# Memory keys issued earlier, memory weights split further ahead, one block's low part by DMA, and the last norm on VectorE alone

## The chip, the cores and the metric

The kernel runs on one core of a Trainium2 chip. The metric is the device time of one execution in microseconds (us); the verdict compares medians over runs on the same chip. Times inside the kernel are read from one profiled execution and count from its first instruction.

## The reference

Two layers of a hybrid decoder step, for 512 prompt tokens and 8 sequences of 8 sample tokens (576 tokens in all), all in float32. Of each layer:

```
rq, rk, rv, rg, sq, sk, sv, mq, g_r, g_s, g_m = in_proj(x, w_in[l])      # x @ w_in, rotary on rq rk sq sk
ret_o = retention(rq, rk, rv);  swa_o = sliding_window_attention(sq, sk, sv, sinks)
mk, mv = mem_prompt @ w_mem_kv[l]                                       # 256 memory tokens, 4 heads of 128
mem_o  = softmax(mq mk^T / sqrt(128)) mv      # prompt; the samples use cache_mem_k, cache_mem_v (8 sequences)
merged = sigmoid(g_r) * (silu(rg) * gn(ret_o)) @ w_br_ret + sigmoid(g_s) * swa_o @ w_br_swa + sigmoid(g_m) * mem_o @ w_br_mem
x = LN(alpha x + merged @ w_out);  h = relu(x @ w_up)^2;  x = LN(alpha x + h @ w_down)
```

## The kernel before

**Tokens and weights.** Tokens stand in the columns, in two groups A and B of 288 (256 prompt, 32 sample each); a group's product of one 128-wide weight unit is 24 matmuls of 288 columns: every weight and every activation is split into a rounded high part (hi) and a remainder (lo), and the three products hi hi, hi lo and lo hi are added. A *unit* is 1024 x 128 weights (512 KB), 154 a layer, in the order of `unit_order()` (line 67): mk 0 to 3 and mv 0 to 3 (keys and values of the memory, with 256 and 512 columns), then retention (rk, rq, rv, rg), sv, sk, sq, the gates gr with br, mq, the gates gs with bs and gm with bm, wo, up, the MLP in quarters (`ua`, `ub`, `dh`) and dn. In the MLP two weight units and two groups are multiplied as a 2 x 2 block with seven products instead of eight (`pair_steps`, line 657); `block()` (line 570) makes the weights of one of the seven, 128 x 512, by sums of VectorE, a cast on ScalarE (hi) and a subtraction on VectorE (lo).

**Buffers and splitting.** Nearly all tiles share one pool of 38 buffers (`N_T`, tag "T"). A tile whose buffer still has readers makes its first writer wait. `run()` (line 613) goes through a stage's steps in order. Between groups of matmuls each step calls `fill.advance(dt)` (line 404), which moves the plan's clock `fill.t`, lets generators (attention, norms) put their next operations into the engines' queues, and then calls `tick()` (line 594), which may split one more unit: its use must be within LOOK = 24 us, the live weight tiles (two a unit, one a block) must not pass `2 * cap`, and it must be due within LEAD = 13 us, or ScalarE free and the data there. `split()` (line 551) takes one of two ways:

```
if self.use[i] - self.fill.t > FAR and k[1] not in ("mq", "gs", "bs", "gm", "bm") and u > 15 \
        and (k[1] != "dh" or k[2] == 0):
    self.nc.scalar.copy(hi, raw)
    self.nc.scalar.activation(lo, raw, AF.Copy, scale=-1.0)
    self.nc.gpsimd.dma_start(lo, raw, accum_op=ALU.add)      # lo = raw - hi, by DMA
else:
    self.split_into(hi, lo, raw, True)                       # cast, and a subtraction on VectorE
```

with FAR = 11. `feed()` fetches raw weights on SP's queue two units ahead of the split. The generators go on when a modelled clock of the engines (`Clock`, line 268) says that their inputs are ready; engines then run their queues in the order of issue, so the model sets the order and the hardware sets the time.

**Attention to the memory.** `mem_prompt` (line 1350) does one head of the prompt: scores, softmax, transposes (line 1389), and the product with the values. `mem_sample` (line 1418) does four of the sample sequences: it makes masked queries, multiplies four key tiles (in_mck, 512 KB each) in turn, then four value tiles (in_mcv). Two key tiles are loaded ahead by `mem_ahead` (line 1414) and two at `mem_sample`'s own start (line 1430), all on GpSimd's queue. The order is prompt head, ahead, prompt head, sample, twice a layer, within the stages gs/bs and the start of gm/bm. Those left over are run off after the first two gm units.

**Norms.** `norm_ev` (line 838) adds each unit's product to a sum, and `last()` (line 883) then takes the mean, the variance and 1/sqrt, and scales. In layer 1's last norm (`out is None`) GpSimd subtracts the mean from half of the columns (line 902) and does the last of four multiplications (line 916), beside VectorE.

**Stages of layer 1's start.** The norm of group B of layer 0 runs while TensorE does mk and mv of layer 1 and then rk and rq of group A; rk of group B is the first that needs it.

Of the kernel before, what the change touches and what calls it, by code (L numbers as in the profile page):

```python
# [43 lines left out]
CAP_M = 4  # L44
# [405 lines left out]
class Builder:  # L450
# [119 lines left out]
    def block(self, u, b):  # L570


        V = self.nc.vector
        ra, rb = self.raw[u - 1], self.raw[u]
        if b == 1:
            sa, sb = self.tile([P, 8, P]), self.tile([P, 4, P], tag=("s", "rc")[u // 2 % 2], bufs=1)
            self.raw[u, "s"] = sa, sb
            V.tensor_tensor(sa.rearrange("p (e s) c -> p e s c", e=2), ra.rearrange("p (e s) c -> p e s c", e=2),
                            rb[:, 0:4].unsqueeze(1).to_broadcast([P, 2, 4, P]), ALU.add)
            V.tensor_tensor(sb, sa[:, 4:8], ra[:, 0:4], ALU.add)  # L580
        elif b > 1:
            sa, sb = self.raw[u, "s"]
        if b == 6:
            V.tensor_tensor(rb[:, 0:4], sb, rb[:, 4:8], ALU.add)
        src = (ra[:, 0:4], b and sb, b and sa[:, 0:4], b and sa[:, 4:8], rb[:, 4:8], ra[:, 4:8], rb[:, 0:4])[b] \
            if b else ra[:, 0:4]
        w = self.tile([P, 8, P], F32R)
        self.nc.scalar.copy(w[:, 0:4], src)
        V.tensor_tensor(w[:, 4:8], src, w[:, 0:4].bitcast(F32), ALU.subtract)
        if b == 6:  # L590
            del self.raw[u - 1], self.raw[u], self.raw[u, "s"]
        return w[:, 0:4], w[:, 4:8]
# [245 lines left out]
    def norm_ev(self, g, y, l, gi, eps, out, scale=None, bias=1.0):  # L838
# [44 lines left out]
        def last():  # L883
            p1, p2 = self.bank("a")[:, :n], self.bank("a")[:, :n]
            yield from mean(p1, st["acc"])
            yield from mean(p2, st["s2"])
            yield (p1,)
            t = self.tile([P, 288], tag="ln", bufs=2)[:, :n]
            S.activation(t, p1, AF.Square)
            mu = p1  # L890
            if out is None:
                mu = self.u(n)
                S.copy(mu, p1)
            yield (t, p2)
            v, r = self.u(n), self.u(n)
            V.scalar_tensor_tensor(v, p2, eps, t, ALU.add, ALU.subtract)
            r0 = self.tile([P, 288], tag="ln", bufs=2)[:, :n]
            S.activation(r0, v, AF.Ln)
            S.activation(r0, r0, AF.Exp, scale=-0.5)
            mb = mu.unsqueeze(1).to_broadcast([P, 4, n])  # L900
            if out is None:
                G.tensor_tensor(y[1], y[1], mb, ALU.subtract)
            V.tensor_tensor(y[0], y[0], mb, ALU.subtract)
            yield (r0,)
            a = self.tile([P, 288], tag="ln", bufs=2)[:, :n]
            V.tensor_tensor(a, r0, r0, ALU.mult)
            V.scalar_tensor_tensor(a, a, -0.5, v, ALU.mult, ALU.mult)
            V.scalar_tensor_tensor(r, a, 1.5, r0, ALU.add, ALU.mult)
            rb = r.unsqueeze(1).to_broadcast([P, 2, n])
            pieces = [(j, slice(k, k + 2)) for j in range(2) for k in (0, 2)]  # L910

            def mult(i):
                j, k = pieces[i]
                if i == 2 and out is not None:
                    V.tensor_tensor(y[1], y[1], mb, ALU.subtract)
                e = G if i == 3 and out is None else V
                e.tensor_tensor(y[j][:, k], y[j][:, k], rb, ALU.mult)
                return y[j][:, k]

            def affine(q, dst, src, eng):  # L920
                gam, bet = gb(q)
                if eng is S:
                    S.activation(dst, src, AF.Identity, scale=gam, bias=bet)
                else:
                    V.tensor_scalar(dst, src, gam, bet, ALU.mult, ALU.add)

            def end(i):
                j, k = pieces[i]
                for q in (k.start, k.start + 1):
                    affine(4 * j + q, y[j][:, q], y[j][:, q], V)  # L930
                h = out[g]["h"][j][:, k]
                self.pick(y[j][:, k], h).tensor_tensor(out[g]["l"][j][:, k], y[j][:, k], h.bitcast(F32), ALU.subtract)
            if out is not None:
                out[g]["h"] += [self.tile([P, 4, n], F32R) for _ in range(2)]
                out[g]["l"] += [self.tile([P, 4, n], F32R) for _ in range(2)]
            z = [mult(i) for i in range(4)]
            step = 1 if out is None else STEP
            wait = ()
            for i in range(0, 4, step):
                yield wait + tuple(z[i:i + step])  # L940
                for j, k in pieces[i:i + step]:
                    for q in (k.start, k.start + 1):
                        affine(4 * j + q, y[j][:, q] if out is None else out[g]["h"][j][:, q], y[j][:, q],
                               V if out is None and i > 1 else S)
                    if out is None:
                        c = 4 * j + k.start
                        nc.sync.dma_start(self.O["yT"][:, c:c + 2, OFF[g]:OFF[g] + n], y[j][:, k])
                    else:
                        wait = (out[g]["h"][j][:, k],)
                if out is not None:  # L950
                    for e in range(i - step, i):
                        if e >= 0:
                            end(e)
            if out is not None:
                yield wait
                for e in range(4 - step, 4):
                    end(e)
            if gi and out is not None:
                for j in range(2):
                    G.dma_start(self.xs[:, 4 * j:4 * j + 4, OFF[g]:OFF[g] + n], y[j])  # L960
# [386 lines left out]
            lo = SW[g]["l"][0][:, :, cs].rearrange("p g (b t) -> p g b t", b=4)  # L1347
            yield from self.hi_lo(hi, lo, o)

    def mem_prompt(self, h, mq, mk, mv, ME):  # L1350
        nc = self.nc
        V, S, T = nc.vector, nc.scalar, nc.tensor
        ident = self.c("ident")
# [33 lines left out]
        for kb in range(2):  # L1387
            for c in range(4):
                T.transpose(pss[kb][:, c * P:(c + 1) * P], p[:, c, kb * P:(kb + 1) * P], ident)
        del p  # L1390
        pT = [self.tile([P, 2, 512], F32R) for _ in range(2)]
        for kb in range(2):
            yield (pss[kb],)
# [24 lines left out]
    def mem_sample(self, kt, l, f, mq, ME):  # L1418
# [8 lines left out]
        for b in range(4):  # L1427
            V.tensor_tensor(qz[:, b], mq[g][:, :, cs],
                            mm[:, b].unsqueeze(1).to_broadcast([P, 4, 32]), ALU.mult)
        kt += [self.mem_load("mck", l, f * 4 + b) for b in (2, 3)]  # L1430
        vt = []
        ps = self.bank("a")
        for b in range(4):
# [43 lines left out]
    def layer(self, l, X):  # L1477
# [30 lines left out]
        def mv_step(i):  # L1508
            def fn():
                if i == 0:  # L1510
                    mvps[0], mvps[1] = self.bank("g"), self.bank("g")
                hi, lo = self.w[uid["mv", i]]
                hi = hi.rearrange("p (k a) c -> p k (a c)", k=2)
                lo = lo.rearrange("p (k a) c -> p k (a c)", k=2)
                for t in range(2):
                    for k in range(2):
                        kk = 2 * i + k
                        xh = M["h"][kk // 4][:, kk % 4, t * P:(t + 1) * P]
                        xl = M["l"][kk // 4][:, kk % 4, t * P:(t + 1) * P]
                        T.matmul(mvps[t], lhsT=xh, rhs=hi[:, k], start=(kk == 0), stop=False)  # L1520
                        T.matmul(mvps[t], lhsT=xh, rhs=lo[:, k], start=False, stop=False)
                        T.matmul(mvps[t], lhsT=xl, rhs=hi[:, k], start=False, stop=(kk == 7))
                    if t == 0:
                        self.fill.advance(6 * mm_us(512))
                if i == 3:
                    for t in range(2):
                        S.copy(mv[:, t, :], mvps[t])
                    nc.gpsimd.dma_start(self.O["mv"][l], mv)
                    nc.gpsimd.dma_start(mvd, mv)
                    nc.gpsimd.dma_start(mkd, mk)  # L1530
            return ([uid["mv", i]], fn, 6 * mm_us(512))
        steps += [mv_step(i) for i in range(4)]

        def mk_out():
# [7 lines left out]
                S.copy(t, ps)  # L1542
                nc.gpsimd.dma_start(self.O["mk"][l, :, kb], t)
        steps.append(([], lambda: self.fill.add(mk_out(), 2), 0.0))
        self.run(steps, CAP_M)

        GR = {g: {"h": [], "l": []} for g in "AB"}
        xs = self.tile([P, 8, P], F32R)
# [175 lines left out]
        mem = []  # L1724
        for f in range(2):
            kt = []
            mem += [self.mem_prompt(2 * f, mq, mk, mv, ME), self.mem_ahead(kt, l, f),
                    self.mem_prompt(2 * f + 1, mq, mk, mv, ME), self.mem_sample(kt, l, f, mq, ME)]
        for gen in mem:
            self.fill.add(gen, 3)  # L1730

# [15 lines left out]
        for i in range(4):  # L1747
            for m in (2 * i, 2 * i + 1):
                steps += self.both(uid["gs", m], X, gate_ev(m))
            for e in range(2):  # L1750
                steps += self.both(uid["bs", i], SW, add_ev(2 * i + e), range(4 * e, 4 * e + 4))
        self.run(steps)
        del SW
        M2 = self.feat_tiles(2)
        y = {}
# [208 lines left out]
```

## Time and profile before

| | us |
|---|---|
| median of three runs | 2178.79 (2178.54 to 2181.57) |
| profiled execution | 2171.27 |
| its span, first to last instruction | 2169.1 |
| TensorE busy in the span | 2118.1 |
| VectorE busy | 1266.0 |
| ScalarE busy | 931.4 |
| GpSimd busy | 236.2 |

A page shares the span among engines; "PE" is TensorE's matmuls, "PEld" its weight loads, DVE VectorE, ACT ScalarE, POOL GpSimd, SP the queue of weight loads. A busy share near 100% says that only the idle time of that engine can be gained. All instructions carry line 359, that of the helper which records them, so one goes by tiles and by place in time: pg and pa are banks of PSUM, T any tile of the common pool, u, t, ln smaller ones.

### The profile page before, as it was taken

The numbers are of one execution on the slowest core, as the hardware profiler recorded it, in microseconds if no ns is written. First come the engines' busy times: TensorE is split into PE (matmuls) and PEld (weight loads), VectorE is DVE, ScalarE is ACT, GpSimd is POOL, SyncE is SP. The second block draws the span as 40 slices with busy tenths as digits, with TensorE's granted clock in tenths as the row PEclk, the third lists the DMA queues.
The fourth block names the chain that finished last, engine by engine and source line by source line (L and its number), as shares of the span: only waits on it lengthen the run. The fifth ranks groups of instructions, "written<-read, shape, count | busy, mean of one in ns | idle before, by whom it ended". The sixth has DMA issues, their size and how long they took to land.

```text
span 2169.1 us, 39184 instructions
## 1 busy us (share of the span) xinstructions
PE 2118.1 (98%) x16180; PEld 2054.7 (95%) x16180; DVE 1266.0 (58%) x2693; ACT 931.4 (43%) x1758; POOL 236.2 (11%) x292
## 2 busy tenths in 40 slices
PE   9999999999999999999989999999999999999997
PEld 8999999989999999999989999999999999999986
DVE  6455544455557576765755556444555575777767
ACT  4333445232256444445543333562231565444452
POOL 0111210000022000000311111010000220000013
PEclk9999999999999999999999999999999999999998
DMA  8455655434375422224775557444342855223241
GB/s 314 114 142 143 166 120 124 137 98 154 109 209 127 125 96 81 79 88 144 198 217 143 143 142 174 118 118 126 126 149 86 228 117 135 88 79 100 95 117 54
DMA packets 86322, 288.75 MB, mean 133 GB/s; under 512 B 9408, under 2 KB 19136, under 8 KB 86080
## 3 DMA queue, kind: packets, MB, share of 16 engines
q1 hardware_dynamic: 50944, 168.27, 23.0%
q0 software_dynamic: 30112, 110.12, 23.0%
q10 hardware_dynamic: 5088, 7.87, 1.1%
q8 instruction: 127, 2.08, 0.4%
q14 instruction: 51, 0.42, 0.1%
HBM read 200.89 MB, written 15.99 MB: 100 GB/s over the span
## 4 chain that ended last, share of the span: by engine, by line
PE 91%; DVE 4%; issue 2%; ACT 2%; DMA 2%; POOL 0%; SPq 0%; DVEq 0%; POOLq 0%; ACTq 0%
PE pg L359 68%; PE pa L359 22%; DVE T L359 3%; ACT T L359 1%; DMA T<-in_wall 1%; ACT u L359 1%; DVE u L359 1%; DMA T<-in_mck 1%; DMA T<-T 0%; DVE ln L359 0%; DVE accA L359 0%; DVE s L359 0%; POOL T L359 0%; ACT t L359 0%; SPq L359 0%
## 5 line engine op out<-in xcount | busy, mean ns | idle before, releaser
L359 PE MATMUL pg<-T,T 128*128 128x288 f32 (+1 forms) x11840 | 1644.1, 297 | 20.4 <-ACT T L359 15.8
L359 PEld LDWEIGHTS pg<-T,T 128*128 128x128 f32 x11840 | 1592.7, 190 | 46.4 <-ACT T L359 23.4
L359 ACT CAST T<-T 128x1024 fp32r<-128x1024 f32 (+7 forms) x483 | 368.7, 788 | 224.0 <-DVE T L359 174.3
L359 PE MATMUL pa<-T,T 128*128 128x288 f32 (+8 forms) x3368 | 447.7, 303 | 10.4 <-DMA T<-in_mck 6.4
L359 PEld LDWEIGHTS pa<-T,T 128*128 128x128 f32 (+3 forms) x3368 | 395.8, 175 | 32.8 <-issue 9.8
L359 DVE TENSOR_TENSOR T<-T,T 128x512 fp32r<-128x512 f32 (+8 forms) x427 | 370.9, 880 | 92.2 <-ACT T L359 82.8
L359 POOL DMA_DIRECT2D T<-T x136 | 118.7, 883 | 1375.4 <-ACT T L359 963.0
L359 ACT ACTIVATE T<-T 128x1024 fp32r<-128x1024 f32 (+1 forms) x148 | 157.5, 1065 | 10.5 <-DVE T L359 8.2
L359 ACT ACTIVATE t<-pg 128x288 f32<-128x288 f32 x128 | 52.7, 411 | 246.7 <-PE pg L359 246.3
L359 ACT ACTIVATE u<-u 128x288 f32<-128x288 f32 x200 | 89.1, 445 | 95.5 <-DVE u L359 91.4
L359 DVE TENSOR_TENSOR T<-u,T 128x288 fp32r<-128x288 f32 x160 | 72.4, 454 | 78.5 <-ACT T L359 78.5
L359 ACT COPY T<-pg 128x512 f32<-128x512 f32 (+2 forms) x44 | 20.9, 480 | 212.3 <-PE pg L359 212.3
L359 DVE TENSOR_TENSOR T<-T,pg 128x288 f32<-128x288 f32 x128 | 57.7, 451 | 73.9 <-PE pg L359 73.6
L359 DVE TENSOR_TENSOR T<-T,u 128x288 f32<-128x288 f32 (+2 forms) x132 | 90.0, 692 | 4.1 <-ACT T L359 0.5
L359 ACT CAST T<-u 128x288 fp32r<-128x288 f32 x160 | 69.3, 433 | 52.6 <-DVE u L359 48.5
L359 DVE SCALAR_TENSOR_TENSOR T<-t,pg 128x288 f32<-128x288 f32 x64 | 29.0, 453 | 93.9 <-ACT t L359 76.2
L359 DVE TENSOR_TENSOR T<-pa,T 128x512 fp32r<-128x512 f32 (+2 forms) x48 | 25.2, 535 | 76.2 <-ACT T L359 75.8
L359 DVE TENSOR_TENSOR T<-T,pa 128x288 f32<-128x288 f32 (+1 forms) x92 | 52.2, 567 | 24.0 <-PE pa L359 23.2
L359 DVE SCALAR_TENSOR_TENSOR u<-t,pg 128x288 f32<-128x288 f32 x64 | 28.7, 448 | 44.1 <-PE pg L359 44.1
L359 DVE TENSOR_TENSOR u<-u,pa 128x288 f32<-128x288 f32 x72 | 32.6, 453 | 33.0 <-PE pa L359 32.8
L359 ACT CAST T<-pa 128x512 fp32r<-128x512 f32 (+2 forms) x40 | 17.4, 437 | 54.1 <-PE pa L359 50.2
L359 DVE CAST T<-T 128x1024 fp32r<-128x1024 f32 (+1 forms) x52 | 35.8, 689 | 6.8 <-PE pa L359 4.8
(165 smaller groups left out, 1107.1 us busy)
## 6 DMA issues: line engine op xcount, KB each, us to landing
T<-in_wall SPq DMA_DIRECT2D x305, 512.0 KB, 4.1
T<-T POOLq DMA_DIRECT2D x136, 512.0 KB, 5.6
T<-in_mck POOLq DMA_DIRECT2D x16, 512.0 KB, 4.4
T<-in_mcv POOLq DMA_DIRECT2D x16, 512.0 KB, 4.7
T<-in_s POOLq DMA_DIRECT2D x8, 512.0 KB, 8.3
out_state_s<-T POOLq DMA_DIRECT2D x8, 512.0 KB, 4.0
T<-in_xT SPq DMA_DIRECT2D x4, 576.0 KB, 11.5
T<-in_xT ACTq DMA_DIRECT2D x4, 576.0 KB, 6.4
```

The source lines that it names most:

```text
L359: r = f(*a, **kw)
```

## The change

In `block()`, block 5 of the last quarter (key q = 7, two pairs a layer) gets its low part from a second ScalarE pass and an accumulating DMA. In `last()`, with `out is None`, GpSimd's subtraction and multiplication go to VectorE. `mem_prompt` gets a function `ahead`, called behind its transposes: the second head of each pair issues key tiles 2 and 3 there, and `mem_sample` no longer does. In `mv_step` `advance` is called after each 3 matmuls, no longer after each 6. The stage of mk and mv has cap 8 in layer 1 (4 in layer 0, as before), and that of gs and bs has cap 2.5, where it had 3.

```diff
@@ block
-        V.tensor_tensor(w[:, 4:8], src, w[:, 0:4].bitcast(F32), ALU.subtract)
+        if b == 5 and self.items[self.split_next][1][2] == 7:
+            self.nc.scalar.activation(w[:, 4:8], src, AF.Copy, scale=-1.0)
+            self.nc.gpsimd.dma_start(w[:, 4:8], src, accum_op=ALU.add)
+        else:
+            V.tensor_tensor(w[:, 4:8], src, w[:, 0:4].bitcast(F32), ALU.subtract)
@@ norm_ev, last
             if out is None:
-                G.tensor_tensor(y[1], y[1], mb, ALU.subtract)
+                V.tensor_tensor(y[1], y[1], mb, ALU.subtract)
...
-                e = G if i == 3 and out is None else V
-                e.tensor_tensor(y[j][:, k], y[j][:, k], rb, ALU.mult)
+                V.tensor_tensor(y[j][:, k], y[j][:, k], rb, ALU.mult)
@@ mem_prompt(..., ahead=None), behind the transposes
+        if ahead is not None:
+            ahead()
@@ mem_sample
-        kt += [self.mem_load("mck", l, f * 4 + b) for b in (2, 3)]
@@ mv_step
                     for k in range(2):
+                        if t or k:
+                            self.fill.advance(3 * mm_us(512))
...
-                    if t == 0:
-                        self.fill.advance(6 * mm_us(512))
...
-            return ([uid["mv", i]], fn, 6 * mm_us(512))
+            return ([uid["mv", i]], fn, 3 * mm_us(512))
...
-        self.run(steps, CAP_M)
+        self.run(steps, 2 * CAP_M if l else CAP_M)
@@ layer
             kt = []
+
+            def more(kt=kt, f=f):
+                kt += [self.mem_load("mck", l, f * 4 + b) for b in (2, 3)]
             mem += [self.mem_prompt(2 * f, mq, mk, mv, ME), self.mem_ahead(kt, l, f),
-                    self.mem_prompt(2 * f + 1, mq, mk, mv, ME), self.mem_sample(kt, l, f, mq, ME)]
+                    self.mem_prompt(2 * f + 1, mq, mk, mv, ME, more), self.mem_sample(kt, l, f, mq, ME)]
@@ layer, the stage of gs and bs
-        self.run(steps)
+        self.run(steps, 2.5)
```

## Rows read from the trace of the kernel before

**Rows 1.** The page's part 1: busy us, share of span, instructions by engine.

```profile
PE 2118.1 (98%) x16180; PEld 2054.7 (95%) x16180; DVE 1266.0 (58%) x2693; ACT 931.4 (43%) x1758; POOL 236.2 (11%) x292
```

**Rows 2.** Waits of TensorE, whole span: us in total, times, longest.

```profile
PE pg L359 <- ACT T L359: 15.8, 9, 4.6
PE pa L359 <- DMA T<-in_mck: 6.4, 2, 3.3
```

**Rows 3.** Windows: busy us by engine, granted clock, DMA share, GB/s.

```profile
1560.40:1572.70 12.30, 9.24 (x67) 7.57 (x67) 2.58 (x6) 2.02 (x4) 2.11 (x4) 0.72 0.71 255
```

**Rows 4.** Timeline of TensorE, first mem_sample, both layers: start, us, [idle before].

```profile
480.96 1.50 PE L359 MATMUL pa<-T,T 128*32 128x256 f32 x24
485.78 1.08 PE L359 MATMUL pa<-T,T 128*32 128x256 f32 x8 [3.32 <-DMA T<-in_mck]
486.79 5.14 PE L359 MATMUL pg<-T,T 128*128 128x288 f32 x30
...
1560.44 1.50 PE L359 MATMUL pa<-T,T 128*32 128x256 f32 x24
...
1566.01 6.38 PE L359 MATMUL pg<-T,T 128*128 128x288 f32 x30
```

**Rows 5.** Timeline of TensorE, undisturbed: second mem_sample's keys, and 30 matmuls.

```profile
536.04 4.23 PE L359 MATMUL pg<-T,T 128*128 128x288 f32 x30
...
547.17 1.93 PE L359 MATMUL pa<-T,T 128*32 128x256 f32 x32
549.03 1.06 PE L359 MATMUL pg<-T,T 128*128 128x288 f32 x6
```

**Rows 6.** Timeline, layer 0: transposes, GpSimd's late key loads; the chain's landing.

```profile
467.44 1.03 PE L359 MATMUL pa<-cst,T 128*128 128x128 f32 x8
...
477.62 0.53 POOL L359 DMA_DIRECT2D T<-in_mck  x1 [26.02 <-DVE T L359]
...
479.99 0.53 POOL L359 DMA_DIRECT2D T<-in_mck  x1 [1.84 <-PE pg L359]
...
479.99 5.75 DMA T<-in_mck
```

**Rows 7.** Timeline of ScalarE and VectorE: the slowest split in gs and bs.

```profile
507.41 1.06 ACT L359 CAST T<-T 128x1024 fp32r<-128x1024 f32 x1
...
511.55 1.22 DVE L359 TENSOR_TENSOR T<-T,T 128x1024 fp32r<-128x1024 f32 x1
```

**Rows 8.** Timeline, layer 0, last quarter's second pair: VectorE, ScalarE, TensorE.

```profile
1011.95 0.69 DVE L359 TENSOR_TENSOR T<-T,T 128x512 fp32r<-128x512 f32 x1 [1.61 <-ACT T L359]
...
1014.85 0.39 ACT L359 COPY u<-pg 128x288 f32<-128x288 f32 x1
...
1015.29 1.86 PE L359 MATMUL pg<-T,T 128*128 128x288 f32 x12 [1.18 <-ACT u L359]
```

**Rows 9.** DMA view: 1059 to 1068 (GpSimd's queue, landing); 1076 to 1102, tenths.

```profile
q0 software_dynamic: 286, 1.04, 63.9%
...
T<-T POOLq DMA_DIRECT2D x3, 512.0 KB, 5.2
...
DMA  7839988679999999999851898993399999899928
```

**Rows 10.** Timeline, layer 1's start: ScalarE's norm and copy, TensorE's wait.

```profile
1079.83 2.17 ACT L359 ACTIVATE T<-T,par 128x288 fp32r<-128x288 f32 x4
...
1089.42 0.37 ACT L359 COPY T<-pg 128x256 f32<-128x256 f32 x1 [1.56 <-PE pg L359]
...
1112.69 2.16 PE L359 MATMUL pg<-T,T 128*128 128x288 f32 x4 [4.61 <-ACT T L359]
```

**Rows 11.** Timeline of VectorE: 1152 columns alone, and the last norm's two steps.

```profile
2110.89 1.36 DVE L359 TENSOR_TENSOR T<-T,u 128x1152 f32<-128x1152 f32 x1
...
2155.24 3.73 DVE L359 TENSOR_TENSOR T<-T,u 128x1152 f32<-128x1152 f32 x1
...
2160.37 3.30 DVE L359 TENSOR_TENSOR T<-T,u 128x576 f32<-128x576 f32 x3
```

More of the change, by code (lines that the diff above doesn't have):

```diff
@@ L1348, in swa_sample, with mem_prompt @@
             yield from self.hi_lo(hi, lo, o)
-    def mem_prompt(self, h, mq, mk, mv, ME):
+    def mem_prompt(self, h, mq, mk, mv, ME, ahead=None):
         nc = self.nc
```

## The prediction

> **What bounds the kernel now.** I read the busy shares first, then TensorE's waits, then its timeline around each wait, then the other engines and the transfers there. TensorE is busy for 2118.1 of 2169.1 us [rows 1]; the change takes no matmul away, so it can only gain or lose idle time of TensorE (some 36 us, all its waits added up) and the slow clock behind it. Two kinds of wait matter here [rows 2]: 6.4 us, in two waits, for memory keys (in_mck), and 15.8 us in nine for tiles that ScalarE writes, the longest 4.6 us. A wait costs more than its length: over the stretch around the second key wait the mean granted clock was 0.72 [rows 3], that is part of it at 1.2 instead of 2.4 GHz.
>
> **Memory keys.** A mem_sample multiplies four key tiles in a row. In layer 0 three of them start at 480.96 (x24) and the fourth only at 485.78 (x8), and the 30 matmuls behind it take 5.14 us; the same in layer 1, with 6.38 us [rows 4]. Undisturbed, in the second mem_sample, the 32 take 1.86 us (547.17 to 549.03) and 30 such matmuls 4.23 [rows 5]. So layer 0 loses 486.79 - 480.96 - 1.86 = 3.97 plus 5.14 - 4.23 = 0.91, together 4.88 us; layer 1 loses 1566.01 - 1560.44 - 1.86 = 3.71 plus 2.15, together 5.86. Sum 10.7.
> The reason stands in GpSimd's rows: the two late key loads go out at 477.62 and 479.99, each held for a buffer, and the last lands 5.75 us after its issue [rows 6]. The change issues both behind the transposes at 467.44 [rows 6], about 10 us before they go out now; even held for one more unit (48 matmuls at the pace of [rows 5], 6.4 us) the last would be there at 467.4 + 6.4 + 5.75 = 479.6, before 480.96. What is late next is the value loads; they take the buffers that the key matmuls free, and then go out at about 482 to 484. The last, 6 us later, is there at 490, about 1.5 us before it is used. I take all of it: **-10.7**. Bounds: 0 if the buffers are no earlier, -10.7.
>
> **cap 2.5 in gs and bs.** Two tiles' worth less of weights may be live, so a unit is split while the one before it runs, 6.4 us ahead, not two units (12.8). One split is a cast and a subtraction; the longest that I see there starts its cast at 507.41 and ends its subtraction at 511.55 + 1.22 = 512.77, so 5.4 us [rows 7], which fits into 6.4 (the low part is wanted 8 or 16 matmuls later still). I take **+0.5**; bounds 0 and, if each of the 24 units (12 a layer) were 0.5 late, +12.
>
> **Low part of block 5, for the last quarter.** Four blocks (two a layer). Each takes a 0.69 us subtraction and its wait of 1.61 us for ScalarE's cast off VectorE, and puts a second ScalarE pass of about 0.61 and an accumulating transfer of 256 KB in their place [rows 8]. In the second pair of the quarter ScalarE and VectorE wait for each other and run behind TensorE, which then waits 1.18 us for the copy at 1014.85 [rows 8]. Laying ScalarE's list out again without the pause: the two activations before it come 0.6 earlier, right behind the added pass, the pre-add of block 6 on VectorE comes out of the way, and the copy moves to about 14.1: 0.7 us a layer. The first pair shows no such wait and gains nothing. **-1.4**. The transfer is issued at about 1012.5 and wanted at 1018.6; from the 512 KB rows below (2.9 us of transfer in 5.2) a half takes 3.7 to 5, so it is just in time. Bounds: -3 and +3 (a miss of 1.5 a layer).
>
> **Memory weights of layer 1.** Here the trace shows no wait of TensorE for them. What the new cap does is in the code: with cap 4, eight tiles are live at the first mk unit, so a unit is split only when one ends, three short units (3 x 24 matmuls of 0.12, 8.6 us) ahead. That is under FAR (11), so hi goes to a cast and lo to VectorE. With cap 8 nothing blocks, and the split comes when LEAD (13) lets it, 12 to 13 us ahead: over FAR. So mv 0 to 3 and the first rk unit move to the path of two ScalarE passes and an accumulating DMA. VectorE loses five subtractions (6 us there, all beside matmuls). The transfers gain five accumulates, each 63.9% of 9 us for 1.04 MB, so 2.9 us of all 16 engines per 512 KB [rows 9]. They fall in the stretch from 1076 to 1102, in which the engines are busy in most slices at 8 or 9 tenths already [rows 9]: 26 us with some 4 to spare, and 14.5 more. The first mv unit starts at about 1089.3, when the last mk is copied out; ScalarE is held by the norm until 1079.83 + 2.17 = 1082.0 [rows 10], so mv 0's pass ends at 1084, its transfer goes out and lands, at the 5.2 us of [rows 9] with a crowd on the engines, at 1089.5 to 91, and its low part is wanted with the second matmul. Letting the transfers share the engines in their order, I get waits of about 1.6, 0.5 and 1.7 us in mv 0 to 2, and a little slow clock: +4.5. On the other side, the norm of group B gets VectorE earlier. Its wait is the longest of all, 4.61 us before the matmuls at 1112.69 [rows 10], because its last steps stand behind the rotary steps of two projections in VectorE's order. The finer advance may let the first of them go ahead; the rest still comes behind projection A. I give that -2. Together **+2.5**; bounds: -6 (that wait and the slow clock in it gone, no transfer late) and +10.6 (all of the transfer time that doesn't fit, 14.5 - 3.9).
> A rule bears on this: the Trainium skill, DMA: Bandwidth & Descriptors, section on the anatomy of one DMA on the SWDGE path, puts a GpSimd transfer at about 2.0 us plus its bytes over 436 GB/s, an estimate of 3.2 us for 512 KB. By it mv 0 would be there at 1088, no low part would be late, and this part would be -2 and not +2.5. The row says 5.2, for accumulates; I go by the row.
> In layer 0 the added advances change nothing that I can see: TensorE waits for nothing there from 18 to 480 us.
>
> **Last norm on VectorE.** At the end VectorE's subtraction of 1152 columns takes 3.73 us beside GpSimd's; alone the same takes 1.36 [rows 11]. Two in a row are 2.7: -1.0. Three multiplications beside GpSimd's take 3.30 [rows 11]; four of 0.72 take 2.9: -0.4. Nothing else runs there: **-1.5**. Bounds -2 and 0. For group B the same steps run under the last matmuls, and VectorE ends them at the same time as now.
>
> **Sum.** -10.7 + 0.5 - 1.4 + 2.5 - 1.5 = -10.6. The profiled execution took 2171.27 us (span 2169.1), so it would be 2160.7; the median of the runs shown is 7.5 higher, 2178.79, and becomes **2168.2**.
>
> **Rivals.**
> (a) *The layer 1 start pays.* The transfers keep up, and group B's norm goes ahead of the rotary steps: -6 in place of +2.5, so -19.1: 2159.7. For it: VectorE's 6 us less there. Against: [rows 9]. The Trainium skill's rule above speaks for it.
> (b) *The keys are no earlier,* since the 38 buffers are still full at the transposes: -10.7 is lost, and the rest makes about 0: 2178.9. For it: both loads wait for buffers now [rows 6]. Against: cap 2.5 leaves two buffers more, just what two loads take.
> (c) *Weights late in gs and bs:* +12 in place of +0.5: 2179.7. Against: the 5.4 us of [rows 7] is the worst of the stretch.
> (d) *Slower: the transfers of the memory weights.* All 10.6 us come out as waits in mv and the first rk, the clock stays at its lower level through some 8 us of matmuls there, as it did around the key waits [rows 3], which doubles them (+8), and the norm of group B, whose steps stand behind those matmuls, moves along: 18.6 in place of 2.5, and the sum +5.5: 2184.3. The other parts give 13.1, so it decides from a price of 17.5 on. For it: the crowd of [rows 9]. Against: a weight that is late holds TensorE, and the transfers behind it are then wanted later too.
>
> **How the numbers follow.** Forecast 58% (2164 to 2174 its own range), (a) 14, (b) 11, (c) 8, (d) 9. About 0.2%, 4.4 us, is what a measurement of this kernel can tell from none. Faster by more than that: the forecast, (a), and some of the milder (c), 0.74; within it: (b), most of (c), 0.16; slower 0.10. Range: (a)'s end at the low side, 2159.5, and most of the way to (b) and (c) at the high side, 2176.5, which leaves out 2 in 10.
>
> **What would show it.** No wait for in_mck on TensorE in either layer, its four key tiles x32 in one piece, and full clock there. GpSimd's key loads just behind the transposes. ScalarE activations in pairs of 1.05 and five more T<-T issues from GpSimd around 1082 to 1096, with waits of TensorE for DMA T<-T in mv if I am right and none if (a) is. From the last group A mean to the end 1.5 us less, with no GpSimd instruction in it. The forecast is wrong if a wait for in_mck stays, or if gs and bs show waits for ScalarE's or VectorE's weight tiles.

## The result, and the profile after

The kernel after takes 2157.77 us (median of four runs, 2157.64 to 2158.67), the kernel before 2179.95 beside it: a ratio of 0.9899, 95% interval 0.9882 to 0.9916, some 22 us. I had forecast 2168.2, about half of that gain, and a range from 2159.5 to 2176.5; the direction was right, the size and the range were not.

The profiled execution of the kernel after took 2157.69 us, its span 2155.9. TensorE's waits (us in total, times, longest) answer to [rows 2]:

```profile
PE pg L359 <- ACT T L359: 10.9, 7, 2.5
PE pg L359 <- DVE T L359: 3.4, 3, 2.1
...
PE pg L359 <- DMA T<-T: 3.2, 2, 2.9
```

The line for in_mck is gone, ScalarE's longest wait has fallen from 4.6 to 2.5, and the waits for accumulating transfers (T<-T) are 3.2 us, where the kernel before had one of 0.2. The window from layer 1's first key matmuls on, as long as that of [rows 3] and nearly at the same place in the work (columns as there), has no wait and the full clock, where it had 0.72:

```profile
1549.00:1561.30 12.30, 12.30 (x159) 11.19 (x152) 7.18 (x21) 2.02 (x4) 2.10 (x4) 1.00 0.69 257
```

The timeline of GpSimd and TensorE at layer 0's first sample (start, us, instruction, idle before) answers to [rows 4, 6]: both late key loads go out 6.5 us ahead of TensorE's transposes (GpSimd doesn't wait for these), and the 32 key matmuls are one piece.

```profile
460.87 1.05 POOL L359 DMA_DIRECT2D T<-in_mck  x2 [9.20 <-PE pg L359]
...
467.33 1.04 PE L359 MATMUL pa<-cst,T 128*128 128x128 f32 x8
...
478.47 1.94 PE L359 MATMUL pa<-T,T 128*32 128x256 f32 x32
```

So far this reads as the prediction said it would. That it is not the work of the moved loads only the experiments show. At layer 1's start TensorE's timeline answers to [rows 10]:

```profile
1085.68 1.22 PE L359 MATMUL pg<-T,T 128*128 128x512 f32 x2 [2.89 <-DMA T<-T]
1086.70 1.16 PE L359 MATMUL pa<-t,ones 128*128 128x288 f32 x4
...
1111.46 0.53 PE L359 MATMUL pg<-T,T 128*128 128x288 f32 x2 [2.06 <-DVE T L359]
1112.94 3.28 PE L359 MATMUL pg<-T,T 128*128 128x288 f32 x13 [0.95 <-DVE T L359]
```

The first line is mv 0's late low part; the last two are what is left of the 4.61 us before group B's rk. The DMA view of 1076 to 1102 (busy tenths; GpSimd's queue; accumulates, median us from issue to landing) answers to [rows 9]:

```profile
DMA  9999996899999999999999999999899999989999
...
q0 software_dynamic: 1230, 4.64, 81.7%
...
T<-T POOLq DMA_DIRECT2D x7, 512.0 KB, 10.7
```

The DMA engines are busy for nine tenths or more in 36 of the 40 slices, and an accumulate takes 10.7 us to land, not 5.2. Last, VectorE's timeline of the end, which answers to [rows 11]:

```profile
2143.94 2.62 DVE L359 TENSOR_TENSOR T<-T,u 128x1152 f32<-128x1152 f32 x2
...
2147.95 2.77 DVE L359 TENSOR_TENSOR T<-T,u 128x576 f32<-128x576 f32 x4
```

Two whole subtractions take 2.62 us where one beside GpSimd took 3.73, and four multiplications 2.77 where three took 3.30.

All kernels here run 16180 matmuls, so their traces can be laid side by side by the number of the matmul. Time in us from one number to another (the columns are runs told below; "before again" is the kernel before profiled a second time, "best" the one with mv 0 and 1 on VectorE, second run):

| matmuls | what | before again | cap 2.5 | cap 2.5 + keys | after | best |
|---|---|---|---|---|---|---|
| 0 to 120 | start | 25.1 | 22.8 | 22.9 | 23.8 | 21.9 |
| 3480 to 4140 | layer 0, first pair and sample | 86.22 | 79.98 | 79.98 | 79.96 | 79.96 |
| 4140 to 4320 | layer 0, second sample's end | 18.00 | 15.73 | 15.72 | 15.73 | 15.73 |
| 7560 to 7840 | layer 0, last quarter, dn | 44.17 | 42.79 | 42.77 | 42.24 | 42.67 |
| 8040 to 8460 | start of layer 1 | 68.06 | 68.00 | 68.02 | 67.67 | 64.73 |
| 11640 to 12100 | layer 1, first pair and sample | 57.66 | 53.17 | 53.17 | 53.12 | 53.12 |
| 12100 to 12480 | layer 1, second sample's end | 45.31 | 42.77 | 42.77 | 42.76 | 42.76 |
| 13500 to 15660 | layer 1, MLP | 288.00 | 288.00 | 288.00 | 288.00 | 288.00 |
| 15660 to 15900 | layer 1, last quarter, dn | 39.20 | 39.39 | 39.39 | 38.10 | 36.57 |
| from the last one on | the last norm | 14.78 | 14.79 | 14.80 | 12.86 | 12.86 |

Two profiles of one kernel differ by up to some 1.6 us in a stage that has waits: in the first profile of the kernel before the two first samples took 84.66 and 58.85 us, in the second 86.22 and 57.66 (143.5 and 143.9 together). TensorE's waits there differ by 0.2 us at most; what differs is the mean granted clock of the stage (0.98 and 0.94 in the first profile, 0.96 and 0.97 in the second).

### The profile page after: what moved, and what is told of

It reads as the page before. It is cut to its first block, busy times and chain, and to the rows that moved or that the text cites. A ratio compares the mean times of both kernels' runs of the same rounds, so it can differ in the third digit from the quotient of the medians.

```text
span 2155.9 us, 39206 instructions
## 1 busy us (share of the span) xinstructions
PE 2118.5 (98%) x16180; PEld 2058.2 (95%) x16180; DVE 1261.5 (59%) x2705; ACT 925.6 (43%) x1750; POOL 232.9 (11%) x297
## 3 DMA queue, kind: packets, MB, share of 16 engines
q1 hardware_dynamic: 50944, 168.27, 22.8%
## 4 chain that ended last, share of the span: by engine, by line
PE 91%; DVE 4%; issue 2%; DMA 2%; ACT 1%; POOL 0%; SPq 0%; DVEq 0%; POOLq 0%; ACTq 0%
PE pg L359 69%; PE pa L359 23%; DVE T L359 3%; DMA T<-T 1%; ACT T L359 1%; DVE u L359 0%; DMA T<-in_wall 0%; ACT u L359 0%; DMA T<-in_memT 0%; SPq L359 0%; DVE ln L359 0%; DVE accA L359 0%; DVE s L359 0%; POOL T L359 0%; POOL rc L359 0%
## 5 line engine op out<-in xcount | busy, mean ns | idle before, releaser
L359 ACT CAST T<-T 128x1024 fp32r<-128x1024 f32 (+6 forms) x464 | 354.6, 789 | 210.1 <-DVE T L359 174.7
L359 DVE TENSOR_TENSOR T<-T,T 128x512 fp32r<-128x512 f32 (+8 forms) x418 | 361.9, 878 | 85.2 <-ACT T L359 75.4
L359 POOL DMA_DIRECT2D T<-T x145 | 124.7, 868 | 1379.2 <-ACT T L359 1013.2
L359 ACT ACTIVATE T<-T 128x1024 fp32r<-128x1024 f32 (+2 forms) x157 | 165.3, 1054 | 10.5 <-DVE T L359 8.2
L359 DVE TENSOR_TENSOR T<-T,pa 128x288 f32<-128x288 f32 (+1 forms) x92 | 52.1, 567 | 25.1 <-PE pa L359 23.7
L359 DVE CAST T<-T 128x1024 fp32r<-128x1024 f32 (+1 forms) x71 | 45.2, 641 | 1.0 <-DMA T<-in_wall 1.0
## 6 DMA issues: line engine op xcount, KB each, us to landing
T<-in_xT SPq DMA_DIRECT2D x4, 576.0 KB, 10.4
```

What stands on the lines that cost most here:

```text
L359: r = f(*a, **kw)
```

## Experiments: which edit gives the time

**The kernel before, again** (no edit).

> The kernel before, unchanged, once more, with a profile of its own. Theory 1: the first profile of it fell on an odd execution: from 1795 to 2075 us its matmuls of 288 columns followed each other every 130 ns, after every 133.3 ns elsewhere and in the kernel after, which is 2160 x 3.3 ns = 7 us, and that is the distance from 2171.3 to the other runs' median of 2178.8. Then this profile shows 133.3 ns there and a span of 2174 to 2179. Rival: the 130 ns belong to the kernel before (its buffers, its order), and the change takes them away; then this profile shows 130 ns there again and a span near 2169, and the 7 us between the profile and the median lie somewhere else. Time against the kernel before: ratio 1.000 by both.

Ratio 1.0004 (0.9995 to 1.0014); the profiled execution took 2182.59 us. The view by windows of TensorE, 1800 to 2070 us (busy us, matmuls, granted clock, DMA share, GB/s), first of the first profile of before, then of this one:

```profile
1800.00:2070.00 270.00, 270.00 (x2080) 1.00 0.31 95
```

```profile
1800.00:2070.00 270.00, 270.00 (x2027) 1.00 0.31 97
```

2080 matmuls against 2027 in the same time, 129.8 ns each against 133.2, with the engine never idle and the granted clock at 1.00 in both. The first profile was an odd execution: from matmul 13500 to 15660 it took 280.8 us, and 288.0 in this and the others of the table. Theory 1 holds: of the 7.5 us between profile and median that stretch is 7.2. So the difference of the two spans, 13.2 us, hides some 7 of the gain.

**Cap 2.5 alone.**

```diff
@@ layer, the stage of gs and bs
-        self.run(steps)
+        self.run(steps, 2.5)
```

> The kernel before with cap 2.5 in gs and bs alone (no key is moved). In the kernel after the waits of TensorE at the end of the second memory sample are gone as well (1.02, 0.38 and 0.36 us at 551 to 553, the same in layer 1), some 2.6 us a layer that I had not counted. Theory: they went because the keys came earlier and the samples' steps with them; then the cap alone changes nothing or costs: 0 to +1 us, both waits for in_mck stay or shrink a little, and the waits at 551 stay. Rival: the cap itself is what frees the buffers; the key loads then go out earlier even without being moved, the in_mck waits fall below half, and the time falls by 5 us or more.

2161.79 us, ratio 0.9919 (0.9906 to 0.9933): 17.8 us faster. My theory was wrong, and the rival's signs are all there. TensorE's and GpSimd's timeline at the first sample, the keys not moved:

```profile
466.33 1.04 PE L359 MATMUL pa<-cst,T 128*128 128x128 f32 x8
467.12 5.04 PE L359 MATMUL pg<-T,T 128*128 128x288 f32 x36
469.43 0.53 POOL L359 DMA_DIRECT2D T<-in_mck  x1 [18.76 <-DVE T L359]
...
473.39 4.15 PE L359 MATMUL pg<-T,T 128*128 128x288 f32 x30
473.62 0.53 POOL L359 DMA_DIRECT2D T<-in_mck  x1 [3.66 <-PE pa L359]
477.46 1.93 PE L359 MATMUL pa<-T,T 128*32 128x256 f32 x32
```

The late loads go out 3.1 and 7.3 us behind the transposes, where they went 10.2 and 12.5 behind them [rows 6]; no key is late. And the order is another: 66 matmuls of units (36 and 30) stand between the transposes and the keys, where 84 stand in the kernel before. Of the same place in "before again":

```profile
471.07 1.03 PE L359 MATMUL pa<-cst,T 128*128 128x128 f32 x8
471.86 4.23 PE L359 MATMUL pg<-T,T 128*128 128x288 f32 x30
...
477.32 7.35 PE L359 MATMUL pg<-T,T 128*128 128x288 f32 x54
484.60 1.50 PE L359 MATMUL pa<-T,T 128*32 128x256 f32 x24
489.60 1.08 PE L359 MATMUL pa<-T,T 128*32 128x256 f32 x8 [3.50 <-DMA T<-in_mck]
```

The whole memory attention moves ahead, and less of its end is left over to be run off in one piece. TensorE at the second sample's end, before again and with cap 2.5:

```profile
556.30 0.44 PE L359 MATMUL pa<-cst,u 128*128 128x128 f32 x2 [1.02 <-ACT u L359]
557.12 0.43 PE L359 MATMUL pa<-T,T 128*32 128x128 f32 x8 [0.38 <-DVE T L359]
557.91 1.74 PE L359 MATMUL pa<-T,T 128*32 128x128 f32 x56 [0.36 <-DVE T L359]
560.12 0.33 PE L359 MATMUL pa<-cst,u 128*128 128x128 f32 x1 [0.47 <-DVE u L359]
```

```profile
544.79 0.38 PE L359 MATMUL pa<-cst,u 128*128 128x128 f32 x2
544.92 1.83 PE L359 MATMUL pg<-T,T 128*128 128x288 f32 x12
546.68 1.95 PE L359 MATMUL pa<-T,T 128*32 128x128 f32 x64
549.11 0.33 PE L359 MATMUL pa<-cst,u 128*128 128x128 f32 x1 [0.48 <-DVE u L359]
```

With cap 3 the sample's steps follow each other with nothing between them, and each is waited for; with cap 2.5 a unit's matmuls stand between them, and only the last is waited for (0.48). By the table: 6.2 and 4.5 us at the two first samples, 2.3 and 2.5 at the second ones, 15.5 in all. Layer 0's last quarter gives another 1.4 (44.17 to 42.79), though TensorE's four waits there are the same (1.2, 1.2, 0.9 and 0.9 us): the mean granted clock of that stage was 0.96 in the three profiles with cap 3 and 1.00 in three with cap 2.5. Why the clock held there no run shows.

**Cap 2.5 and the moved keys.** The edit of `mem_prompt`, `mem_sample` and `layer` as in the change, and the cap.

> The kernel before with the keys issued at the transposes and cap 2.5, nothing else of the change. As the prediction has it: -10.7 + 0.5 = -10.2 us, the waits for in_mck gone and those at 551 and 1632 unchanged. By the trace of the kernel after: the first memory sample gains 4.4 and 5.9 us, the end of the second sample 2.7 and 2.5 more, -15.5 us in all, a ratio of 0.9929, with the waits at 551 and 1632 (but the last, 0.48) gone. If those belong to another part of the change, -10 and the waits stay.

2162.25 us, ratio 0.9922 (0.9908 to 0.9935). In every stage of the table it equals cap 2.5 alone within 0.1 us, but for the start by chance. The loads go out earlier, at 460.03 and not at 469.43 and 473.62, and nobody waits for them in either. The move is worth nothing on top of the cap. The move without the cap was not run, so what it would give alone stays open.

**Cap 2.5 with two buffers fewer.**

```diff
-N_T = 38
+N_T = 36
```

> The kernel with cap 2.5 alone (2161.8 us, no wait for in_mck), but with 36 buffers in the common pool, not 38, everywhere. Theory: what the cap gives is two free buffers at the moment at which the key loads want one; two buffers fewer take them away again, so at the first memory sample of each layer GpSimd's late key loads go out under 9 us before the fourth key matmuls again, TensorE waits 2 to 4 us for in_mck, and the waits at the end of the second sample (1.0, 0.4, 0.4) are back or larger. Rival: what helps is that weights are split later, which takes ScalarE and VectorE work out of the way of the samples' steps; then the buffers don't matter, and no wait for in_mck comes back. The whole time is not to be compared, since all other stages have fewer buffers too.

One execution, 2190.64 us, which is not to be compared. On every engine the instructions stand in the same order as with cap 2.5 and 38 buffers; only buffers are scarcer. GpSimd and TensorE at the first sample of layer 0, then a line from layer 1:

```profile
478.20 1.04 PE L359 MATMUL pa<-cst,T 128*128 128x128 f32 x8
...
485.72 1.05 POOL L359 DMA_DIRECT2D T<-in_mck  x2 [20.95 <-PE pa L359]
489.33 1.50 PE L359 MATMUL pa<-T,T 128*32 128x256 f32 x24
491.11 0.64 PE L359 MATMUL pa<-T,T 128*32 128x256 f32 x8 [0.27 <-DMA T<-in_mck]
...
501.67 0.65 PE L359 MATMUL pa<-T,T 128*32 128x128 f32 x16 [0.87 <-DMA T<-in_mcv]
...
1586.52 0.64 PE L359 MATMUL pa<-T,T 128*32 128x128 f32 x16 [2.22 <-DMA T<-in_mcv]
```

Half a miss for each theory. The loads go out later again, 7.5 and 8.0 us behind the transposes (3.1 and 7.3 with 38 buffers), as the buffers' theory says. But the key wait is 0.27, not 2 to 4; the values wait instead (0.87 and 2.22); and the second sample's end stays at 15.72 and 42.77 us. First samples: 81.49 and 55.95. So of the cap's 15.5 us the order keeps 4.7, 1.7, 2.3 and 2.5, that is 11.3, with the buffers as scarce as that, and the two buffers are worth the other 4.3. This is one profile against one, so the parts are good to a microsecond or so. The two orders differ in more than the steps' places: with cap 2.5 VectorE has 17 instructions more and ScalarE 17 fewer. No run separates these.

## Experiments: the other parts

**Memory weights of layer 1 alone** (finer advance and cap 8).

> The kernel before with the finer advance in mv and cap 8 for the memory weights of layer 1, nothing else. The prediction has +2.5 us for it (late low parts in mv +4.5, group B's norm -2). The trace of the kernel after shows in layer 1 a wait of 2.9 us for an accumulating transfer at 1085.7 and slow clock behind it, and group B's norm wait down from 4.6 and 0.6 to 2.1 and 1.0; from the last matmuls of layer 0 to 1138 it stands 0.3 us ahead of the kernel before, and 2.3 us behind it after the first 25 us of layer 0. Theory 1: the 2.3 are chance at the start (the first transfers), so this kernel is within 1 us of before. Theory 2: the finer advance costs 2.3 at layer 0's start, so +2.

2179.94 us, ratio 1.0005 (0.9994 to 1.0015): nothing, as theory 1 had it; the start of layer 0 took 22.2 us, less than in "before again", so that was chance. TensorE at layer 1's start:

```profile
1094.35 0.72 PE L359 MATMUL pg<-T,T 128*128 128x512 f32 x2 [2.22 <-DMA T<-T]
...
1102.47 7.89 PE L359 MATMUL pg<-T,T 128*128 128x512 f32 x29 [1.85 <-DMA T<-T]
...
1121.54 0.53 PE L359 MATMUL pg<-T,T 128*128 128x288 f32 x2 [2.06 <-DVE T L359]
1123.02 4.22 PE L359 MATMUL pg<-T,T 128*128 128x288 f32 x19 [0.94 <-DVE T L359]
```

It pays 4.1 us for late low parts. Before rk of group B TensorE waits 3.0 us, where "before again" waits 5.6 (4.61, 0.56, 0.45), and the mean granted clock of the stage is 0.95 and not 0.92; so the stage is only 0.6 us longer.

**The kernel after with cap 4 again in layer 1.**

```diff
-        self.run(steps, 2 * CAP_M if l else CAP_M)
+        self.run(steps, CAP_M)
```

> The kernel after with cap 4 for the memory weights of layer 1 again; the finer advance stays. No memory value weight then goes by an accumulating transfer. Theory 1: group B's norm comes earlier because of the finer advance; then its wait before rk of group B stays near 2 and 1 us, no wait for transfers in mv, 3 us faster than the kernel after (2154.5). Theory 2, the prediction's other reason: VectorE, freed of five subtractions, makes the norm earlier; then the wait is back at 4.6 and 0.6 us and the time within 1 us of the kernel after.

2157.64 us beside 2157.07 for the kernel after on the same chip (e9, below). As theory 2 said, with cap 4 the wait is back, finer advance or not. TensorE:

```profile
1087.54 0.43 PE L359 MATMUL pa<-t,ones 128*128 128x288 f32 x2
...
1096.39 0.43 PE L359 MATMUL pa<-t,ones 128*128 128x288 f32 x2
...
1106.24 2.17 PE L359 MATMUL pg<-T,T 128*128 128x288 f32 x4 [4.62 <-ACT T L359]
```

The two pairs of matmuls with ones give group B's mean and its squares. Here the second pair comes 8.9 us behind the first; in the kernel after all four stand together at 1086.70. So the cap brings the norm forward. Theory 2's reason, VectorE freed of subtractions, is not shown by this: the cap also places the splits earlier, and the run with all four mv on VectorE, below, speaks against it.

**mv 0 and 1 of layer 1 back on VectorE.**

```diff
@@ split
-                and (k[1] != "dh" or k[2] == 0):
+                and (k[1] != "dh" or k[2] == 0) and (k[1] != "mv" or k[2] > 1):
```

> The kernel after, but mv 0 and mv 1 of layer 1 are split with VectorE's subtraction and not by an accumulating transfer. In the kernel after TensorE waits 2.9 us for mv 0's low part, issued at 1077.4 and landed at 1085.6 (8.2 us, DMA engines full in nearly every slice), while VectorE idles 6.9 us from 1081 to 1088; group B's mean, behind those matmuls, comes 2.9 us later and its norm is waited for by 2.1 and 1.0 us. Theory: the two subtractions fit into VectorE's idle time, the wait for the transfer goes, the norm comes 2.9 earlier, and the transfers behind come earlier for two fewer: -3 to -4 us with the slow clock, 2154 to 2155 us. Rival: TensorE then only arrives earlier at group B's norm, which waits for the rotary steps in VectorE's order as before: 0 to -1, and the wait before rk of group B grows by what mv lost.

2151.39 us (2147.86 to 2154.28), ratio 0.9879 (0.9861 to 0.9897). It scatters, and its profiled run (2147.86) has a stretch with short matmuls in layer 0's MLP, so I ran it again beside the kernel after:

> The kernel after, unchanged, once more, beside the next three on one chip. 2157.8 again. Some runs 7 us lower if stretches with 130 ns a matmul (in place of 133.3) come by chance in any kernel, as they did in 2 of 21 runs of the kernel before (2171 and 2172 us against 2177 to 2183) and in the profile of the kernel with mv 0 and 1 on VectorE (728 to 1000 us); none lower if such a stretch belongs to certain kernels.

> The kernel after with mv 0 and mv 1 of layer 1 on VectorE, once more, now beside the kernel after on one chip. In its first profile the start of layer 1 (from the 7840th to the 8360th matmul) is 3.3 us shorter than in the kernel after, and its runs lay between 2147.9 and 2154.3, the profiled one with a stretch of 130 ns a matmul that takes 7 us off. So 3.3 us faster than the kernel after in runs without such a stretch: 2154.5, and 2147 to 2148 in runs with one.

The kernel after: 2157.07 (2151.36 to 2158.84; one of four runs is 6 us low, so such runs seem to come in this kernel too, though no trace shows it). With mv 0 and 1 on VectorE: 2151.88 (2151.55 to 2152.48), ratio to before 0.9869 (0.9855 to 0.9884), the best version here. TensorE at layer 1's start:

```profile
1083.77 0.69 PE L359 MATMUL pa<-t,ones 128*128 128x288 f32 x4
...
1090.56 3.58 PE L359 MATMUL pg<-T,T 128*128 128x512 f32 x17 [0.39 <-DMA T<-T]
...
1095.73 8.26 PE L359 MATMUL pg<-T,T 128*128 128x288 f32 x60 [0.45 <-DMA T<-T]
1105.93 0.67 PE L359 MATMUL pg<-T,T 128*128 128x288 f32 x2 [1.94 <-DVE T L359]
1107.40 4.93 PE L359 MATMUL pg<-T,T 128*128 128x288 f32 x19 [0.80 <-DVE T L359]
```

VectorE does the two subtractions and one step of the norm from 1074.61 on, in 3.03 us. Low parts are late by 0.8 us in all and not 3.2, group B's norm moves ahead with them, and the stage is 2.9 us shorter (64.73 against 67.67), or 3.5 against the kernel after's second profile (68.22). The runs give 5.2. Another 1.5 of it shows at 15660 to 15900 (36.57 against 38.09): TensorE's two waits there are the same (1.2 and 2.5 us), but the mean granted clock is 1.00 and not 0.96. The cap 4 kernel's profile has that too (36.58) and its runs are no faster for it; that stays open.

**All four mv on VectorE** (the same line, with every mv left out).

> The kernel after with cap 8 kept, but all four mv units of layer 1 split with VectorE's subtraction; mk 3 and rk 0 still by transfer. Theory: VectorE has room for four (it idles 6.9 us there in the kernel after), no transfer is late and SP's loads come earlier: as with two, or 0.5 us better, 2154. Rival: four subtractions push group B's norm back, its wait before rk of group B grows from 1.8 towards 4.6: 2155 to 2157.

2156.69 us (2155.26 to 2156.95): no better than the kernel after, though its profile has the start of layer 1 at 65.33 and a span of 2153.1. TensorE at layer 1's start:

```profile
1086.01 0.43 PE L359 MATMUL pa<-t,ones 128*128 128x288 f32 x2
...
1088.33 0.43 PE L359 MATMUL pa<-t,ones 128*128 128x288 f32 x2
...
1106.18 0.53 PE L359 MATMUL pg<-T,T 128*128 128x288 f32 x2 [0.94 <-DVE T L359]
1107.71 0.53 PE L359 MATMUL pg<-T,T 128*128 128x288 f32 x2 [1.00 <-DVE T L359]
1109.19 3.11 PE L359 MATMUL pg<-T,T 128*128 128x288 f32 x12 [0.94 <-DVE T L359]
```

The rival's reason does not show: with four of the five subtractions back on VectorE the second pair with ones comes 2.3 us behind the first, not 8.9, and the waits before rk of group B are 2.9 us together, against 3.0 in the kernel after and 5.6 with cap 4. So what brings group B's norm forward is for the most part not VectorE's relief. It comes with the higher cap, by the earlier splits or by the one subtraction that is still gone; no run separates these two. Against the kernel after's second profile this one loses 1.8 us at 12480 to 13500 (144.41 against 142.64), which takes back a part of the stage's gain; why the runs are no better is not settled.

**Block 5 by DMA, and the last norm, each with cap 2.5.** The edits as in the change.

> Cap 2.5 and the low part of block 5 by DMA, nothing else. Against cap 2.5 alone (2161.8, PE waits of 1.19 for a copy at 1009.5 and of 1.18 at 2079.8). The prediction has -0.7 a layer, so 2160.4. By the trace of the kernel after, the wait is 0.09 and gone, 1.1 a layer, of which layer 0 gives 0.8 back in two short waits for dn's weights near 1030, whose transfers come 0.5 us later: so -1.1 to -1.9, 2160 to 2160.7.

2160.98 us against 2161.79: -0.8, a little less than expected, and not clear of noise (the ranges, 2160.24 to 2161.52 and 2161.15 to 2163.34, overlap, and the two ran on different chips, on which the kernel before took 2179.26 and 2179.56). The trace is clearer. The wait of 1.2 us for the copy is gone in both layers. In layer 1 the stage takes 38.09 us and not 39.39. In layer 0 it takes 42.89 and 42.79, nothing, because the mean granted clock of the stage was 0.96 here and 1.00 with cap 2.5 alone.

> Cap 2.5 and the last norm on VectorE alone, nothing else. Against cap 2.5 alone (2161.8). The prediction has -1.5, so 2160.3; the traces of cap 2.5 and of the kernel after, from the last wait of TensorE (for accA) to the end, stand 15.6 and 13.7 us apart from it: -1.9 and -0.2 for that wait, -2.1, so 2159.7.

2162.38 us (2158.80 to 2163.30): these runs scatter too much to tell 2 us. The trace does: from the last matmul on 12.85 us and not 14.79, and from matmul 15900 to the last one 39.07 and not 39.37, together -2.2.

## Why the prediction was right in direction and wrong in size

- **The step that failed is the cap**: +0.5, with bounds 0 and +12. I saw it only as less lead for the weights, and shut out a gain without a reason. It measured -17.8 us. With the lower cap the plan splits later (around layer 0's memory attention most casts of weights start 35 to 85 matmuls further on), and the memory attention's steps, key loads among them, stand earlier in TensorE's order. That order was most of the gain (11.3 of 15.5 us in the four stages), and two freer buffers the rest. That the later splits are what moves the steps is my reading of the plan; no run shows it by itself.
- **Memory keys, -10.7**: the size of the loss was read rightly (6.2 and 4.5 us at the two first samples, 10.7 together; 10.4 against the profile that I had read), and it went. That the number came true was luck as far as the cause goes: it was not the moved loads, which are worth 0 on top of the cap. I had written that the cap leaves just the two buffers that the loads want, but used it only as an argument against rival (b) and never priced it by itself.
- **What stood behind the key waits**: 2.3 and 2.5 us at the second samples' ends. Nothing in the prediction priced them; the waits of 1.0, 0.4 and 0.4 us were in the trace.
- **Memory weights, +2.5**: 0.4 by the runs of that part alone. Late low parts came as forecast (2.22 and 1.85 us alone, 2.89 in the kernel after). What came back with group B's norm is more than the 2 us that I gave it: some 3.5, since 4.1 were lost and the stage is only 0.6 longer (68.66 against 68.06). The reason "finer advance" for it is refuted by the cap 4 kernel (4.62 us again), and the reason that the norm "gets VectorE earlier" is not borne out by the kernel with all four mv on VectorE, where most of the gain stays (2.9 us of waits against 5.6). It comes with the cap of 8. In the kernel after mv 0's transfer goes out at 1077.39 and TensorE waits for it until 1085.68. The Trainium skill, DMA: Bandwidth & Descriptors, section on the anatomy of one DMA on the SWDGE path, gives an estimate of 3.2 us for it; the trace does not agree (8.3 here, 10.7 in the median of the stretch), and the measurement decides. Rival (a), for which that rule spoke, did not come.
- **Block 5, -1.4**: -0.8 by the runs. The wait for the copy, 1.18 us a layer, went but for 0.09, where I had counted on 0.7 of it; TensorE's next one, 1.19 us for VectorE, stayed. By the trace of that part alone layer 1 gains 1.3 and layer 0 nothing, since the granted clock of its stage fell to 0.96.
- **Last norm, -1.5**: -2.2 by the traces. Subtractions 1.1, multiplications 0.5, the rest in small waits around them and ahead of them.
- **From profile to median, +7.5**: right: 7.2 of it is the first profile's odd stretch, which is not in the median.

Sum of what was measured (medians, for the last norm traces): -17.8 + 0 - 0.8 + 0.4 - 2.2 = -20.4, of 22.

## What to carry to other kernels

Where a change lowers a limit so that another edit can work, price the limit by itself, on both sides of zero: in a kernel whose order comes from a plan, it moves every instruction that the plan places behind it. Test the enabling edit alone before crediting the edit that it enables. When an edit does two things at once, as cap 8 did (earlier splits, and work moved from VectorE to transfers), undo one of them alone before naming the cause: here it was not the one that I had named. Moving work to transfers paid here only while the transfers had room; two of the five subtractions back on VectorE, which idled, kept the gain and dropped most of the cost (5.2 us by the runs), while all four of mv back gave nothing by the runs.

## What the hardware showed besides

- Matmuls of 288 columns follow each other every 133.2 ns, but in some executions every 129.8 for a whole MLP stage, 7 us, with the granted clock at 1.00 in both. Two profiles show it, in different layers and kernels; 4 of the 37 runs of the kernel before that were timed beside the experiments stand apart in the same way (2171.0 to 2172.4, the others from 2177.4 on), though no trace shows those. What sets it off stays open.
- The same waits can cost 1.3 to 1.5 us more or less by whether the granted clock falls behind them. At 15660 to 15900, with the same two waits of TensorE (1.2 and 2.5 us), the stage took 38.09 us at a mean granted clock of 0.96 in both profiles of the kernel after, and 36.56 to 36.58 at 1.00 in the four profiles of its three variants with fewer or no mv transfers. What decides it stays open.
- Of the seven accumulates of 512 KB that the kernel after issues from 1076 to 1102, at layer 1's start, the slowest landed 12.74 us after its issue; over the whole profile the median was 5.7.
